# Where the search for the next part to begin ahead starts: at the part just split, or one past it

## The chip, the cores and the metric

One core of a Trainium2 chip runs the kernel. The metric is the device time of one execution in microseconds (us), and each row below is from one profiled execution. The engines are TensorE (PE: matmuls; PEld: its weight loads), VectorE (DVE), ScalarE (ACT), GpSimd (POOL) and SyncE (SP), which issues most of the DMAs.

## The reference

A decoder layer in float32 on 256 tokens of width 2048, with the rows of the two outer lines twice the size of the rest:

```python
x = x + 0.5 * swiglu(rms_norm(x, g_ffn1), w_gu1, w_down1)   # w_gu: 2048 x 2*5632, w_down: 5632 x 2048
x = x + hybrid_mixer(rms_norm(x, g_mix), ...)               # gated conv, windowed attention, w_o
x = x + 0.5 * swiglu(rms_norm(x, g_ffn2), w_gu2, w_down2)

def swiglu(h, w_gu, w_down):
    g, u = jnp.split(h @ w_gu, 2, axis=-1)
    return (jax.nn.silu(g) * u) @ w_down
```

## The kernel before

Each weight is read once, by SP, in **groups** of 128 x 2048 float32 (1 MB) into the tile `raw`, of which there are three. A group is cut into **parts** of at most 1024 columns. Each part is split into two tiles of the rounded type fp32r, `hi` (ACT copies it, L102) and `lo` = source minus `hi` (DVE subtracts, L103), and PE makes each product of three matmuls of 512 columns: x_hi*hi (L486), x_hi*lo (L487), x_lo*hi (L488).

The two SwiGLU half-steps run over 11 units of 512 columns of gate and up, in blocks of 4, 4 and 3; after each block come two down products. A unit has 8 pairs of 128-row blocks of the contraction. A pair is plain (`p`: two parts, eight products) or is made with seven products (`s`: sums of blocks first, four parts). `PLAN = "sppspspp"` sets this for units 2 to 10 (unit 2 in the order `FIRST`), `DOWN` for the down products; unit 0 is plain, and unit 1 has groups marked `q`. The four parts of an `s` group are taken in this order: `u` and `d`, 1024 columns each of sums that DVE makes from `raw` (L174 to L176); `a`, 1024 columns straight from `raw`; and `r`, 512 columns from `raw`. PE takes three products' worth of 512 columns less for them than for a plain pair, and DVE has the three sums more to do.

`Feed.take` hands PE its next part. Before that it goes on splitting parts as long as there are buffers: three `hi`/`lo` pairs in the pool `wsplit` (`BUFS`), one more in a late pool (`MORE`). So instructions of parts three or four ahead stand on ACT and DVE between those of the part at hand and the rest of the work. Other work is put in between from a list (`posts`, `pending`): the transposed activations (`act`, with the sums `rf` and `aforms`, for the down products), and at the end of a unit the **folds**: L544 to L548 gather what the seven products left, L552 to L555 add it to the four halves of the two PSUM tiles `mm`, L556 is silu, L558 the product. The next unit's third product writes into `mm` and so waits for L552 and L553.

There is a second way to split a part, meant for form `a` and for the second parts of `q` groups, with two buffers of its own (`ADDED`), which `take` does not count among the four:

```python
nc.scalar.copy(hi, src)                               # L185, tile ahi
nc.scalar.activation(lo, src, AF.Copy, scale=-1.0)    # L186, tile alo
nc.gpsimd.dma_start(lo, src, accum_op=ALU.add)        # L187, alo += src in the DMA
self.ready[i] = hi, lo, w, self.parts[i][3]
self.added += 1
```

`ahead(i)`, called right after part `i` was split in the ordinary way, looks from `begun` on for such a part in this group, or also in the next one when `i` isn't the first of its own. `added` goes down only when a part that `take` found ready is done with; where the part begun is `i` itself, its buffers are counted as ordinary ones and `added` stays up. With `added` at two, nothing is begun any more.

Of the kernel before, what the change touches and what calls it, by code (L numbers as in the profile page):

```python
# [56 lines left out]
def hybrid_layer(ctx: ExitStack, tc: tile.TileContext, a: dict, out: bass.AP):  # L57
# [67 lines left out]
    class Feed:  # L125
# [64 lines left out]

        def ahead(self, i):

            self.begun = max(self.begun, i)
            g = self.parts[i][0]
            first = i == 0 or self.parts[i - 1][0] != g
            for j in range(self.begun, min(i + 9, len(self.parts))):
                if self.parts[j][0] > g + (not first) or self.added == ADDED or not self.pool:
                    break
                self.begun = j + 1
                if self.parts[j][5] == "a":  # L200
                    self.begin(j)
# [840 lines left out]
```

## Time and profile before

| | |
|---|---|
| median of 3 runs (lowest to highest) | 2178.42 us (2176.48 to 2183.15) |
| profiled execution: time; span of its instructions | 2180.23 us; 2178.4 us |
| mean granted clock of PE | 0.977 |
| busy share: PE, DVE, ACT, POOL | 95%, 78%, 51%, 3% |
| parts begun ahead (L187 instructions) | 6 |

The rows take 0 to 800 us for the first half-step, 800 to 1440 for the mixer and its borders, and 1440 to the end for the second, less what little of it lies before. PE's busy time counts pipelined matmuls, so its idle time is a lower bound of what it loses, and a matmul at a lower granted clock counts as busy.

### The profile page before, as it was taken

How to read it: one execution, taken by the hardware profiler on the slowest of the kernel's cores; microseconds unless marked ns; L12 is line 12 of the kernel's file. 1: busy time of each engine (PE TensorE's matmuls, PEld its weight loads, DVE VectorE, ACT ScalarE, POOL GpSimd, SP SyncE). 2: the span in 40 equal slices, each digit the busy share in tenths (PEclk: the TensorE clock that was granted, in tenths of full speed). 3: DMA queues.
4: the chain of work that ended last, by engine and by line, in shares of the span. 5: the costliest groups of instructions: out<-in, count | busy, mean ns of one | idle time of the engine just before them, and what ended most of it. 6: DMA issues, size and time to landing. Idle time of an engine off the chain costs nothing. (4 is left out here: it accounts for less than half of the span.)

```text
span 2178.4 us, 24482 instructions
## 1 busy us (share of the span) xinstructions
PE 2067.9 (95%) x9482; PEld 1689.7 (78%) x9482; DVE 1689.0 (78%) x1912; ACT 1101.1 (51%) x1338; POOL 69.6 (3%) x61
## 2 busy tenths in 40 slices
PE   8889999999999999999999999998999999999998
PEld 7667787777877778887888888886778777787777
DVE  5678888888988874568766665658888888988887
ACT  5545555554555454455545444544544545545553
POOL 1000000000000000621000000000000000000000
PEclk9999999999999999999999999999999999999999
DMA  6655455444554445443555555554454545454444
GB/s 235 208 182 187 174 199 195 177 184 155 213 184 164 174 174 193 168 142 116 193 183 187 192 193 183 185 186 152 173 185 174 213 154 186 178 197 181 185 156 154
DMA packets 58230, 392.84 MB, mean 180 GB/s; under 512 B 6913, under 2 KB 8065, under 8 KB 12033
## 3 DMA queue, kind: packets, MB, share of 16 engines
q1 hardware_dynamic: 57104, 388.10, 49.3%
q0 software_dynamic: 864, 3.15, 0.8%
q8 instruction: 74, 1.21, 0.2%
q14 instruction: 44, 0.35, 0.1%
q10 hardware_dynamic: 144, 0.02, 0.0%
HBM read 386.00 MB, written 2.10 MB: 178 GB/s over the span
## 5 line engine op out<-in xcount | busy, mean ns | idle before, releaser
L103 DVE TENSOR_TENSOR lo<-raw,hi 128x1024 fp32r<-128x1024 f32 (+1 forms) x725 | 848.4, 1183 | 388.7 <-ACT hi L102 376.3
L102 ACT CAST hi<-raw 128x1024 fp32r<-128x1024 f32 (+1 forms) x725 | 718.5, 1000 | 498.4 <-PE mm L488 217.4
L486 PE MATMUL mm<-hi,h 128*128 128x512 f32 x955 | 380.5, 398 | 36.1 <-DVE v L553 31.3
L487 PE MATMUL mm<-lo,h 128*128 128x512 f32 x955 | 377.5, 395 | 8.0 <-DVE lo L103 7.9
L488 PE MATMUL mm<-hi,h 128*128 128x512 f32 x955 | 376.7, 394 | 0.0
L102 ACT CAST hi<-u 128x1024 fp32r<-128x1024 f32 x172 | 181.5, 1055 | 313.4 <-DVE u L174 275.9
L486 PEld LDWEIGHTS mm<-hi,h 128*128 128x128 f32 x955 | 181.9, 191 | 83.4 <-DVE v L553 36.6
L103 DVE TENSOR_TENSOR lo<-u,hi 128x1024 fp32r<-128x1024 f32 x172 | 210.1, 1222 | 13.8 <-ACT hi L102 10.0
L487 PEld LDWEIGHTS mm<-lo,h 128*128 128x128 f32 x955 | 181.9, 191 | 48.9 <-DVE lo L103 13.3
L488 PEld LDWEIGHTS mm<-hi,h 128*128 128x128 f32 x955 | 181.7, 190 | 38.7 <-DVE h L325 0.6
L486 PE MATMUL mm<-hi,act 128*128 128x512 f32 x512 | 202.8, 396 | 3.2 <-DVE v L555 1.9
L487 PE MATMUL mm<-lo,act 128*128 128x512 f32 x512 | 200.7, 392 | 0.0
L488 PE MATMUL mm<-hi,act 128*128 128x512 f32 x512 | 200.3, 391 | 0.0
L283 PE MATMUL gate<-h,hi 128*128 128x512 f32 x512 | 181.0, 396 | 0.0
L285 PE MATMUL gate<-h,lo 128*128 128x256 f32 x480 | 134.6, 280 | 0.0
L486 PEld LDWEIGHTS mm<-hi,act 128*128 128x128 f32 x512 | 97.2, 190 | 28.0 <-issue 4.4
L283 PEld LDWEIGHTS gate<-h,hi 128*128 128x128 f32 x512 | 96.0, 188 | 22.0 <-issue 0.8
L488 PEld LDWEIGHTS mm<-hi,act 128*128 128x128 f32 x512 | 96.9, 189 | 20.5
L487 PEld LDWEIGHTS mm<-lo,act 128*128 128x128 f32 x512 | 97.0, 189 | 19.7
L174 DVE TENSOR_TENSOR u<-raw 128x1024 f32<-128x1024 f32 x86 | 104.9, 1219 | 0.0
L283 PE MATMUL xc<-h,hi 128*128 128x512 f32 x256 | 93.1, 406 | 0.0
L285 PEld LDWEIGHTS gate<-h,lo 128*128 128x128 f32 x480 | 90.7, 189 | 0.7
(258 smaller groups left out, 3013.2 us busy)
## 6 DMA issues: line engine op xcount, KB each, us to landing
raw<-in_w_gu SPq DMA_DIRECT2D x172, 1024.0 KB, 4.6
raw<-in_w_down SPq DMA_DIRECT2D x88, 1024.0 KB, 4.7
raw<-in_w_mix SPq DMA_DIRECT2D x56, 1024.0 KB, 5.1
raw<-in_w_o SPq DMA_DIRECT2D x16, 1024.0 KB, 4.8
raw<-in_w_qkv SPq DMA_DIRECT2D x12, 1024.0 KB, 4.8
raw<-in_w_oc SPq DMA_DIRECT2D x8, 1024.0 KB, 4.8
raw<-in_w_oa SPq DMA_DIRECT2D x8, 1024.0 KB, 4.8
raw<-in_w_gu SPq DMA_DIRECT2D x7, 512.0 KB, 6.7
```

What stands on the lines that cost most here:

```text
L102: nc.scalar.copy(dst[0], src)
L103: nc.vector.tensor_tensor(dst[1], src, dst[0].bitcast(F32), op=ALU.subtract)
L174: nc.vector.tensor_tensor(u[:, :2], b[:, 0:4:3], b[:, 1:2].broadcast_to([P, 2, NCH]), op=ALU.add)
L283: nc.tensor.matmul(ps[:, b], whi, both, start=k == 0, stop=last)
L285: nc.tensor.matmul(ps[:, b, :S], wlo, x[:, k, 0], start=False, stop=False)
L486: nc.tensor.matmul(ps, x[0], hi, start=name not in self.begun, stop=False)
L487: nc.tensor.matmul(ps, x[0], lo, start=False, stop=False)
L488: nc.tensor.matmul(ps, x[1], hi, start=False, stop=last)
```

## The change

`ahead` begins its search one part later, so that it never begins the part that has just been split:

```diff
         def ahead(self, i):
 
-            self.begun = max(self.begun, i)
+            self.begun = max(self.begun, i + 1)
             g = self.parts[i][0]
             first = i == 0 or self.parts[i - 1][0] != g
             for j in range(self.begun, min(i + 9, len(self.parts))):
```

Two of the six parts begun before were the part at hand (in units 1 and 2 of the first half-step), and after them `added` stood at two for good. Now none is, and 94 parts are begun, 47 in each half-step, nearly all of the 102 of that kind. Past unit 1 each stands 6 to 8 parts ahead of the one that PE takes then.

ACT, where unit 7 of the second half-step goes over into the first down product (`g<-p` is the gather, `act` the turned activations, `hi<-u` the parts `u` and `d`, 1024 columns of `raw` the parts `p` and `a`, 512 columns `r`). Before:

```order
L544 COPY g<-p_13719 128x512
L102 CAST hi<-raw 128x1024
L102 CAST hi<-u 128x1024
L102 CAST act<-at 128x2x256
L102 CAST hi<-u 128x1024
L102 CAST act<-at 128x2x256
L102 CAST hi<-raw 128x1024
L556 ACTIVATE g<-g 128x1024
L102 CAST hi<-raw 128x512
```

And of the change:

```order
L544 COPY g<-p_13778 128x512
L102 CAST hi<-raw 128x1024
L185 CAST ahi<-raw 128x1024
L186 ACTIVATE alo<-raw 128x1024
L102 CAST hi<-u 128x1024
L102 CAST act<-at 128x2x256
L102 CAST hi<-u 128x1024
L185 CAST ahi<-raw 128x1024
L186 ACTIVATE alo<-raw 128x1024
L102 CAST act<-at 128x2x256
L102 CAST hi<-raw 128x512
L556 ACTIVATE g<-g 128x1024
```

Ahead of `hi<-u` stand two more instructions, for the `a` of this group, and behind the second `hi<-u` two for the `a` of the next; the copy of `a` in front of silu (L556) is gone, and that of `r` has moved ahead of silu.

DVE at the same place. Before:

```order
L103 TENSOR_TENSOR lo<-u,hi 128x1024
L103 TENSOR_TENSOR act<-at,act 128x2x256
L103 TENSOR_TENSOR lo<-u,hi 128x1024
L103 TENSOR_TENSOR act<-at,act 128x2x256
L103 TENSOR_TENSOR lo<-raw,hi 128x1024
L552 TENSOR_TENSOR g<-g,mm 128x512
L553 TENSOR_TENSOR v<-mm,v 128x512
L554 TENSOR_TENSOR g<-g,mm 128x512
L555 TENSOR_TENSOR v<-mm,v 128x512
L103 TENSOR_TENSOR lo<-raw,hi 128x512
L558 SCALAR_TENSOR_TENSOR g<-g,v 128x1024
L174 TENSOR_TENSOR u<-raw 128x1024
```

And of the change:

```order
L103 TENSOR_TENSOR lo<-u,hi 128x1024
L103 TENSOR_TENSOR act<-at,act 128x2x256
L103 TENSOR_TENSOR lo<-u,hi 128x1024
L103 TENSOR_TENSOR act<-at,act 128x2x256
L103 TENSOR_TENSOR lo<-raw,hi 128x512
L552 TENSOR_TENSOR g<-g,mm 128x512
L553 TENSOR_TENSOR v<-mm,v 128x512
L554 TENSOR_TENSOR g<-g,mm 128x512
L555 TENSOR_TENSOR v<-mm,v 128x512
L174 TENSOR_TENSOR u<-raw 128x1024
L175 TENSOR_TENSOR u<-u,raw 128x512
L176 TENSOR_TENSOR u<-u,raw 128x512
```

The subtraction for `a` in front of the folds (L552 to L555) is replaced with the shorter one for `r`, and the sums for the next group (L174) follow at once on the folds; L558 comes later.

DVE, where unit 4 of the second half-step goes over into unit 5. Before:

```order
L103 TENSOR_TENSOR lo<-u,hi 128x1024 x2
L103 TENSOR_TENSOR lo<-raw,hi 128x1024
L552 TENSOR_TENSOR g<-g,mm 128x512
L553 TENSOR_TENSOR v<-mm,v 128x512
L554 TENSOR_TENSOR g<-g,mm 128x512
L555 TENSOR_TENSOR v<-mm,v 128x512
L103 TENSOR_TENSOR lo<-raw,hi 128x512
L558 SCALAR_TENSOR_TENSOR g<-g,v 128x1024
L103 TENSOR_TENSOR lo<-raw,hi 128x1024 x4
```

And of the change:

```order
L103 TENSOR_TENSOR lo<-u,hi 128x1024 x2
L103 TENSOR_TENSOR lo<-raw,hi 128x512
L552 TENSOR_TENSOR g<-g,mm 128x512
L553 TENSOR_TENSOR v<-mm,v 128x512
L554 TENSOR_TENSOR g<-g,mm 128x512
L555 TENSOR_TENSOR v<-mm,v 128x512
L103 TENSOR_TENSOR lo<-raw,hi 128x1024
L558 SCALAR_TENSOR_TENSOR g<-g,v 128x1024
L103 TENSOR_TENSOR lo<-raw,hi 128x1024 x3
```

Again `r` stands ahead of the folds in the place of `a`, and the first plain part of the next group comes ahead of L558.

## Rows read from the trace of the kernel before

**Rows 1.** The page: the chain that ended last, by engine.
```profile
PE 22%; DVE 7%; ACT 1%; issue 1%; ACTq 0%
```

**Rows 2.** Stretches: us, busy us by engine (x instructions), granted clock, DMA share, GB/s.
```profile
140.00:800.00 660.00, 623.51 (x2695) 503.98 (x2694) 571.14 (x621) 338.42 (x382) 0.00 (x0) 0.97 0.50 183
800.00:1440.00 640.00, 636.86 (x3355) 535.36 (x3354) 397.44 (x469) 319.17 (x447) 55.45 (x42) 1.00 0.51 177
1440.00:1510.00 70.00, 61.34 (x258) 49.52 (x257) 55.51 (x80) 33.19 (x44) 0.00 (x0) 0.93 0.37 136
1510.00:2178.00 668.00, 627.21 (x2698) 506.74 (x2696) 572.36 (x617) 333.64 (x367) 0.00 (x0) 0.97 0.49 180
```

**Rows 3.** PE waiting for whom: us in total, times, longest us.
```profile
PE mm L486 <- DVE v L553: 32.5, 14, 4.9
PE p L486 <- ACT hi L102: 16.2, 6, 2.7
PE p L487 <- DVE lo L103: 13.1, 17, 0.9
PE mm L487 <- DVE lo L103: 7.9, 8, 1.7
...
PE gu L487 <- DMA alo<-raw: 5.6, 4, 2.7
```

**Rows 4.** DVE in order of time: start us, us, operation; [idle before <- releaser].
```profile
1761.55 0.68 DVE L545 TENSOR_TENSOR g<-g,p 128x512 f32<-128x512 f32 x1
...
1776.95 1.22 DVE L103 TENSOR_TENSOR lo<-raw,hi 128x1024 fp32r<-128x1024 f32 x1 [0.26 <-ACT hi L102]
1778.10 0.68 DVE L552 TENSOR_TENSOR g<-g,mm 128x512 f32<-128x512 f32 x1
```

**Rows 5.** ACT in order of time around the same place.
```profile
1747.76 1.06 ACT L102 CAST hi<-raw 128x1024 fp32r<-128x1024 f32 x1 [0.30 <-PE mm L488]
...
1760.28 0.58 ACT L544 COPY g<-p 128x512 f32<-128x512 f32 x1
...
1766.78 1.06 ACT L102 CAST hi<-u 128x1024 fp32r<-128x1024 f32 x1 [4.97 <-DVE u L174]
...
1775.88 1.04 ACT L102 CAST hi<-raw 128x1024 fp32r<-128x1024 f32 x1
```

**Rows 6.** PE in order of time, two matmuls that waited.
```profile
1879.05 0.50 PE L486 MATMUL p<-hi,aforms 128*128 128x512 f32 x1 [2.69 <-ACT hi L102]
1880.48 0.80 PE L487 MATMUL p<-lo,aforms 128*128 128x512 f32 x1 [0.93 <-DVE lo L103]
```

**Rows 7.** DVE in order of time at that place.
```profile
1874.88 0.69 DVE L103 TENSOR_TENSOR lo<-raw,hi 128x512 fp32r<-128x512 f32 x1 [1.04 <-ACT hi L102]
...
1876.62 1.22 DVE L174 TENSOR_TENSOR u<-raw 128x1024 f32<-128x1024 f32 x1
```

**Rows 8.** Short stretches, columns as in Rows 2.
```profile
1778.00:1785.00 7.00, 5.57 (x13) 4.25 (x14) 5.97 (x9) 4.55 (x6) 0.00 (x0) 0.51 0.24 84
1829.20:1832.60 3.40, 3.40 (x10) 2.60 (x8) 2.83 (x3) 3.40 (x5) 0.00 (x0) 0.50 0.32 87
1872.00:1880.50 8.50, 4.35 (x17) 2.30 (x15) 7.34 (x11) 3.71 (x5) 0.00 (x0) 1.00 0.35 123
2008.00:2016.00 8.00, 6.68 (x29) 5.05 (x28) 7.38 (x7) 4.39 (x6) 0.00 (x0) 1.00 0.64 229
```

**Rows 9.** Tile alo: xcount, duration ns min/median/max, first and last start us; landing.
```profile
L186 ACT ACTIVATE alo<-raw x6: 1048/1059/1069, 55.8 to 124.3; 128x1024 fp32r<-128x1024 f32 x6
...
DMA to landing us min/median/max: 4.5/4.6/7.7
```

**Rows 10.** POOL in order of time, one of the six issues.
```profile
77.10 0.85 POOL L187 DMA_DIRECT2D alo<-raw  x1 [16.23 <-ACT alo L186]
```

**Rows 11.** DVE in order of time beside it.
```profile
77.04 0.69 DVE L357 TENSOR_TENSOR rn<-h 128x512 f32<-128x512 f32 x1
```

**Rows 12.** PE in order of time, a matmul on the `lo` of `a`.
```profile
1757.98 0.39 PE L487 MATMUL mm<-lo,h 128*128 128x512 f32 x1
```


## The prediction

> **What bounds the kernel now.** I read the page first, then the stretches, then the waits of PE, then single places. PE is busy 95% of the span, yet 7% of the span lies on DVE in the chain that ended last, and 1% each on ACT and on issue [rows 1]. By stretches PE loses almost nothing in the mixer (636.86 of 640.00 us busy at clock 1.00), and much in the half-steps: 660.00 - 623.51 = 36.5 us idle from 140 to 800, 668.00 - 627.21 = 40.8 from 1510 on, at a mean clock of 0.97 in both [rows 2]. The clock has two levels, 2.4 and 1.2 GHz; a mean of 0.97 is worth 0.03 x 660 = 20 us in the one and as much in the other. So some 77 us of idleness and 40 us of slow clock are there to be had, besides the first units of each half-step (0 to 140 and 1440 to 1510).
>
> The waits say who ends this idleness. The four rows with DVE and ACT sum to 32.5 + 16.2 + 13.1 + 7.9 = 69.7 us [rows 3], nine tenths of the 77. They fall on the same twelve places in each half-step: where one unit follows another, where the down products follow a unit, and where the second down product follows the first. The reason is to be seen at one of them: DVE goes from the gather at 1761.55 through sums, subtractions and activations, and comes to the subtraction for `a` at 1776.95 and to the folds only at 1778.10 [rows 4]; the longest wait for L553, 4.9 us, ends there. ACT meanwhile stands idle 4.97 us ahead of 1766.78 for DVE's sums [rows 5].
>
> **What the change removes and adds.** 94 parts less 6 are begun ahead. Each takes a subtraction of 1.22 us from DVE [rows 4] and gives ACT 1.06 us more (L186; L185 stands for the L102 that goes), 0.85 us to POOL [rows 10], and a DMA of 512 KB that lands 4.5 to 7.7 us after its issue [rows 9]. Summed, DVE loses 88 x 1.22 = 107 us and ACT gains 93, but only what stands ahead of a PE wait counts, since elsewhere DVE and ACT wait for buffers anyway. ACT's extra two instructions mostly stand right ahead of `hi<-u`, where it idles for DVE's sums (4.97 us against 2.1), so there I cost them at nothing; without that cover each would delay `hi<-u` by 2.1 us.
>
> *Unit to unit with activations turned, eight places* (of the 32.5 us 4.9 at four places and about 2.9 at four; the other six waits are of 0.2). The copy and subtraction for `r` (0.69 us for the subtraction, at 1874.88 [rows 7]; the copy of 512 columns I set at 0.6, a little over half of 1.04) stand in the place of 1.04 and 1.22 for `a`. `hi` of `r` can start when ACT is done with `act`, 1775.88 + 0.1, DVE is free about 1776.7, so the folds start near 1777.25 and not at 1778.10: 0.85 us. Besides, `a` no longer holds one of four buffers, so the plain parts behind it are split one small part (1.36 us of PE) earlier, and the gather L545 follows not on three subtractions (1761.55) but on ACT's copy, which ends at 1760.86 [rows 4, 5]: 0.7 us more. That gives 1.55 each, 12.4 us; 0.85 each (6.8) if the second does not pass through.
>
> *Into the down products, six places.* From 1872 to 1880.5 PE is idle 8.50 - 4.35 = 4.15 us [rows 8], 2.69 and 0.93 of it in two waits [rows 6]. The long one is for `u` of the next `s` group, whose sums start at 1876.62, behind `r` (itself behind silu, at 1874.88) and L558 [rows 7]. Now the sums follow on the folds at once: 1876.62 - 3.3, and ACT's `hi` of it comes after silu at about 1875.7, when PE arrives. Against this, here alone two extra ACT instructions stand ahead of `act`, and with it of the folds: 2.1 us of ACT, all but 0.25 of it beside DVE's own work ahead of the folds; the earlier gather takes 0.7 off. What I then count at this place is about 0.3 for L555, 1.1 for `lo` of `u` and 1.0 for `lo` of `d`, which now stands behind L558: 2.4 us. Gain 1.75 each, 10.5 us; 1.05 each (6.3) without the earlier gather.
>
> *Second down product, six places* (0.9 us each, within the 13.1) and *unit to unit with nothing turned, four places* (from 2008 on 8.00 - 6.68 = 1.3 us idle [rows 8], most of the 7.9 [rows 3]). In the first 1.22 us leaves the chain ahead of the late `lo`; in the second `r` and L558 (0.69 + 1.22) no longer stand between the folds and the late `lo`. Both waits are shorter than what leaves (L558 runs 1.22 us, as the subtraction does), so they go: 5.4 + 5.2 = 10.6 us.
>
> *First units.* In the first half-step PE waited 5.6 us for `alo` in unit 1 [rows 3], on parts begun at hand or four parts ahead; now the nearest are five ahead. But two that had left DVE come back to it. I take 4. In the second half-step 8.7 us are idle from 1440 to 1510 [rows 2], and four subtractions (4.9 us) leave DVE there, against four more ACT instructions in a chain that goes to and fro between the two: I take 3. Sum 7, bounds 0 and 5.6 + 4.9 = 10.5.
>
> *Clock.* After the wait of 4.9 us PE ran 7 us at clock 0.51, after one of 2.9 us 3.4 us at 0.50; across the 1.3 us it stayed at 1.00 [rows 8]. So the 2.9 us places, at about 1.4 us, should stay at full clock, the 4.9 us ones at 3.4 should do as the 2.9 ones did, and the down places, in pieces of about 1 us, may go either way. I take half of the 40 us back, 20; bounds 0 and 30.
>
> *Late landings.* The tightest place in the steady part is the third `s` group of a unit. PE wants `lo` of `a` at 1757.98 [rows 12]. `ahi` would follow on the copy that starts at 1747.76 [rows 5], or 1.36 us earlier with the buffer freed one part earlier: 1.06 + 2.1 us later POOL issues, at 1750.9 or 1749.6, and a landing after 7.7 us is at 1758.6 or 1757.3: 0.6 us late, or in time. After 4.5 us it is in time either way. DMA is at a share of 0.50 [rows 2], so many landings will share the engines with a load of `raw`; I expect 5 to 8 us, and set 3 us for late ones at these 18 places; bounds 0 and 18 x 0.6 = 11. The loads of `raw` themselves are slowed too, but they go out two groups ahead.
>
> **Sum.** 12.4 + 10.5 + 10.6 + 7 + 20 - 3 = 57.5 us off 2180.2, the profiled execution's own time (0.08% over the median of the runs): 2123. Of the bounds, 6.8 + 6.3 + 10.6 + 0 + 0 - 11 = 13 give 2167, and 12.4 + 10.5 + 10.6 + 10.5 + 30 - 0 = 74 give 2106.
>
> **Rivals.** *The waits shorten but the clock does not come along, or landings eat part of it:* 13 to 30 us, 2150 to 2167. For it: the pieces that stay at the down places add up, and the 4.9 us places remain over 3. Chance 0.20.
>
> *Nothing moves:* the folds are late for ACT's activations and not for `a`, and PE waits as before; 2178. Against it: at 1776.95 the subtraction for `a` is the last thing ahead of the folds, and it is gone. Chance 0.06.
>
> *Slower: `alo` lands after PE wants it.* The four waits on it in unit 1 took 5.6 us, 1.4 each [rows 3]. If the accumulating DMAs and the loads hold each other up so that half of the 94 parts wait 1.4 us, that is 66 us against the gain of 57 (and the slow clock comes with such waits): 2190 to 2210. It decides from about 0.6 us a part, which at the tightest place means landings of 9 us, 1.3 over the longest seen. Chance 0.09.
>
> A rule speaks for this one: the Trainium skill, "SBUF — State Buffer", section "SBUF: two separate sides", says that GpSimd writes the descriptors of a DMA issued from its queue through ports that it shares with VectorE, and is locked out while certain VectorE instructions run, so that such a DMA waits for descriptors. By it, with DVE busy 86% of the half-steps, each landing would be put off by an instruction or two of DVE, 1.2 to 2.4 us: at the 18 tight places up to 1.7 us late, 31 us, so 2154. By this trace it doesn't hold for the instructions that DVE runs here: the issue at 77.10 fell 0.06 us into a DVE instruction with two SBUF inputs and another followed [rows 10, 11], and it took the usual 0.85 us. I leave it 0.03.
>
> **Chances and range.** The forecast (2106 to 2150) gets 0.62, the partial gain 0.20, the lock 0.03, no move 0.06, slower 0.09. Range 2100 to 2168, which leaves out no change and slower, and a little at the bottom. About 0.3%, 6.5 us, is what a measurement here can tell from nothing: faster 0.85, same 0.06, slower 0.09.
>
> **What would show it.** The subtraction L103 from `raw` is run 88 times less and L187 94 times. Each landing of `alo` within 8 us and PE's waits on it under 5 us in all. The waits on L553 fall from 32.5 to about 19 us, those on `hi` (16.2) to near nothing, those on `lo` in plain matmuls (7.9) too. The mean clock rises from 0.977 to about 0.985. I am wrong if PE's waits on `alo` go into tens of us, if ACT's extra copies appear ahead of `hi<-u` in PE's waits, or if PE's idle time falls and the clock doesn't rise.

## The result, and the profile after

The changed kernel takes 2112.29 us (median of 3 runs, 2107.99 to 2114.93) against 2178.42: a ratio of 0.969, interval 0.9654 to 0.9725, 66 us faster. Timed again (x_after, on a chip numbered 10; the chip of the first timing isn't on record) it took 2124.07 us (4 runs, 2119.46 to 2128.66; ratio 0.9747, 0.973 to 0.9764), where the kernel before took 2179.23. The forecast of 2123 and its range hold for both. The profiled execution of the first took 2114.93 us, with a span of 2113.1 us at a mean granted clock of 0.990 (0.977 before).

The page of the changed kernel: busy time by engine, the two large DMA queues (packets, MB, share of 16 engines), and the chain that ended last, which answers to [rows 1]:

```profile
PE 2044.4 (97%) x9482; PEld 1675.5 (79%) x9482; DVE 1586.0 (75%) x1822; ACT 1178.5 (56%) x1424; POOL 145.4 (7%) x149
...
q1 hardware_dynamic: 57104, 388.10, 51.3%
q0 software_dynamic: 13536, 49.29, 12.7%
...
PE 66%; DVE 15%; DMA 8%; ACT 5%; issue 5%; POOL 1%; SPq 0%; ACTq 0%; POOLq 0%; DVEq 0%
```

DVE is 103 us less busy than before (1689.0), ACT 77 us more (1101.1). PE's idle time (span less busy time) fell from 2178.4 - 2067.9 = 110.5 to 68.7 us, and its busy time by 23.5. The share of DVE and DMA in the chain has grown all the same: the chain goes back through whatever released each step, at no matter how small a wait, and so its shares are no measure of loss.

Stretches of the changed kernel, columns as in [rows 2, 8]; the last two lie behind the fold's wait at a change of unit with activations turned, and at a change to the down products:

```profile
140.00:800.00 660.00, 641.33 (x2825) 522.21 (x2825) 537.96 (x603) 391.11 (x450) 34.40 (x40) 0.99 0.71 223
800.00:1400.00 600.00, 596.86 (x3175) 502.19 (x3174) 376.98 (x437) 296.20 (x415) 55.50 (x42) 1.00 0.51 177
1400.00:1480.00 80.00, 72.42 (x303) 57.54 (x303) 58.61 (x84) 44.15 (x55) 5.16 (x6) 0.96 0.62 191
1480.00:2113.00 633.00, 608.48 (x2673) 494.50 (x2671) 516.99 (x568) 366.72 (x403) 35.25 (x41) 0.99 0.70 221
1732.60:1736.00 3.40, 3.18 (x8) 2.44 (x8) 1.94 (x3) 3.40 (x4) 0.00 (x0) 0.51 0.53 222
1823.00:1831.00 8.00, 6.43 (x25) 4.17 (x24) 7.93 (x10) 6.64 (x8) 0.00 (x0) 1.00 0.48 160
```

From 140 to 800 PE is idle 18.7 us where it was 36.5, and 24.5 us in the second half-step behind its first units where it was 40.8; the mixer's 3.1 us are as before. The DMA engines' share has risen from 0.50 to 0.71.

Who PE waits for in the changed kernel (us, times, longest), to be set against [rows 3]:

```profile
PE mm L486 <- DVE v L553: 19.1, 8, 3.8
PE p L487 <- DVE lo L103: 9.5, 13, 0.9
PE p L486 <- ACT g L566: 7.0, 2, 3.6
PE mm L487 <- DMA alo<-raw: 6.9, 8, 1.8
PE mm L487 <- DVE lo L103: 4.4, 5, 1.8
...
PE gu L487 <- DMA alo<-raw: 0.6, 2, 0.4
```

The 16.2 us on `hi` in the down products are gone. DVE in order of time at one change of unit, and then at one change to the down products, which answer to [rows 4, 7]:

```profile
1729.24 0.69 DVE L103 TENSOR_TENSOR act<-rn,act 128x512 fp32r<-128x512 f32 x1
1729.85 0.68 DVE L103 TENSOR_TENSOR lo<-raw,hi 128x512 fp32r<-128x512 f32 x1
1730.45 0.68 DVE L552 TENSOR_TENSOR g<-g,mm 128x512 f32<-128x512 f32 x1
...
1823.05 0.68 DVE L555 TENSOR_TENSOR v<-mm,v 128x512 f32<-128x512 f32 x1
1823.65 1.21 DVE L174 TENSOR_TENSOR u<-raw 128x1024 f32<-128x1024 f32 x1
...
1826.24 1.22 DVE L103 TENSOR_TENSOR lo<-u,hi 128x1024 fp32r<-128x1024 f32 x1
1827.37 1.22 DVE L558 SCALAR_TENSOR_TENSOR g<-g,v 128x1024 f32<-128x1024 f32 x1
```

And PE there, with one of the new waits on a landing:

```profile
414.29 0.50 PE L487 MATMUL mm<-alo,h 128*128 128x512 f32 x1 [1.83 <-DMA alo<-raw]
...
1731.78 0.50 PE L486 MATMUL mm<-hi,h 128*128 128x512 f32 x1 [3.84 <-DVE v L553]
...
1827.51 0.50 PE L487 MATMUL p<-lo,aforms 128*128 128x512 f32 x1 [0.92 <-DVE lo L103]
...
1829.78 0.50 PE L487 MATMUL p<-lo,aforms 128*128 128x512 f32 x1 [0.60 <-DVE lo L103]
```

The short subtraction for `r` stands ahead of the folds now, the sums for the next group begin 0.6 us after L555 does, and what is left at the down place is 1.57 us where it was 4.15. Tile `alo` of the changed kernel, as in [rows 9]:

```profile
L187 POOL DMA_DIRECT2D alo<-raw x94: 850/859/1018, 57.3 to 2074.2; - x94
...
DMA to landing us min/median/max: 4.5/6.7/10.3
```

### The profile page after: what moved, and what is told of

Same layout as the page of the kernel before. It is cut to its first block, busy times and chain, and to the rows that moved or that the text cites. A ratio compares the mean times of both kernels' runs of the same rounds, so it can differ in the third digit from the quotient of the medians.

```text
span 2113.1 us, 24661 instructions
## 1 busy us (share of the span) xinstructions
PE 2044.4 (97%) x9482; PEld 1675.5 (79%) x9482; DVE 1586.0 (75%) x1822; ACT 1178.5 (56%) x1424; POOL 145.4 (7%) x149
## 3 DMA queue, kind: packets, MB, share of 16 engines
q0 software_dynamic: 13536, 49.29, 12.7%
## 4 chain that ended last, share of the span: by engine, by line
PE 66%; DVE 15%; DMA 8%; ACT 5%; issue 5%; POOL 1%; SPq 0%; ACTq 0%; POOLq 0%; DVEq 0%
PE mm L487 11%; PE mm L488 11%; PE mm L486 11%; PE gate L283 6%; DVE lo L103 5%; DMA alo<-raw 5%; PE yo L283 3%; PE gate L285 3%; ACT hi L102 2%; DMA raw<-in_w_gu 2%; PE p L487 2%; PE xc L283 2%; PE p L488 2%; PE p L486 2%; PE bg L283 2%
## 5 line engine op out<-in xcount | busy, mean ns | idle before, releaser
L103 DVE TENSOR_TENSOR lo<-raw,hi 128x1024 fp32r<-128x1024 f32 (+1 forms) x635 | 742.1, 1177 | 397.8 <-ACT hi L102 387.4
L102 ACT CAST hi<-raw 128x1024 fp32r<-128x1024 f32 (+1 forms) x635 | 623.6, 990 | 484.3 <-PE mm L488 192.3
L486 PE MATMUL mm<-hi,h 128*128 128x512 f32 x902 | 358.0, 397 | 23.1 <-DVE v L553 19.1
L487 PE MATMUL mm<-lo,h 128*128 128x512 f32 x902 | 354.5, 393 | 4.9 <-DVE lo L103 4.4
L488 PE MATMUL mm<-hi,h 128*128 128x512 f32 x902 | 354.3, 393 | 0.0
L102 ACT CAST hi<-u 128x1024 fp32r<-128x1024 f32 x172 | 181.2, 1054 | 161.8 <-DVE u L174 117.1
L486 PEld LDWEIGHTS mm<-hi,h 128*128 128x128 f32 x902 | 171.4, 190 | 63.3 <-DVE v L553 22.5
L103 DVE TENSOR_TENSOR lo<-u,hi 128x1024 fp32r<-128x1024 f32 x172 | 209.9, 1220 | 13.4 <-ACT hi L102 10.3
L488 PEld LDWEIGHTS mm<-hi,h 128*128 128x128 f32 x902 | 170.8, 189 | 36.2 <-DVE h L325 0.4
L187 POOL DMA_DIRECT2D alo<-raw x94 | 81.0, 862 | 1686.7 <-ACT alo L186 1611.6
L486 PE MATMUL mm<-hi,act 128*128 128x512 f32 x480 | 187.8, 391 | 0.0
L488 PE MATMUL mm<-hi,act 128*128 128x512 f32 x480 | 186.9, 389 | 0.0
L487 PE MATMUL mm<-lo,act 128*128 128x512 f32 x480 | 186.8, 389 | 0.0
L488 PEld LDWEIGHTS mm<-hi,act 128*128 128x128 f32 x480 | 90.1, 188 | 18.8
L486 PEld LDWEIGHTS mm<-hi,act 128*128 128x128 f32 x480 | 90.1, 188 | 18.6 <-DVE v L553 0.2
L174 DVE TENSOR_TENSOR u<-raw 128x1024 f32<-128x1024 f32 x86 | 104.7, 1217 | 0.0
L185 ACT CAST ahi<-raw 128x1024 fp32r<-128x1024 f32 x94 | 98.5, 1048 | 5.1 <-DMA raw<-in_w_gu 3.7
```

Source lines behind the costliest of these rows:

```text
L102: nc.scalar.copy(dst[0], src)
L103: nc.vector.tensor_tensor(dst[1], src, dst[0].bitcast(F32), op=ALU.subtract)
L174: nc.vector.tensor_tensor(u[:, :2], b[:, 0:4:3], b[:, 1:2].broadcast_to([P, 2, NCH]), op=ALU.add)
L486: nc.tensor.matmul(ps, x[0], hi, start=name not in self.begun, stop=False)
L487: nc.tensor.matmul(ps, x[0], lo, start=False, stop=False)
L488: nc.tensor.matmul(ps, x[1], hi, start=False, stop=last)
```

## The experiments

The question is what made the time: the subtractions that DVE is rid of (relief), or the two buffers that `take` doesn't count, by which six parts and not four can be in hand (depth). Every edit is to the changed kernel. Four kernels ran on each of three chips; the kernel before took 2178.42, 2178.71 and 2179.23 us there. Times are medians of at least four runs (of three in the first two rows); idle is PE's span less its busy time in the profiled run.

| label | what is different | us | ratio to before, interval | clock | idle us | PE's waits on alo, us |
|---|---|---|---|---|---|---|
| (before) | | 2178.42 | | 0.977 | 110.5 | 8.9 |
| (after) | the change, first timing | 2112.29 | 0.9654 to 0.9725 | 0.990 | 68.7 | 7.5 |
| x_none | nothing begun ahead | 2173.53 | 0.9968 to 0.9986 | 0.977 | 104.2 | 0 |
| x_depth | begun ahead, DVE subtracts | 2127.78 | 0.9753 to 0.9782 | 0.989 | 80.9 | 0 |
| x_counted | begun parts count among the four (98 begun) | 2143.02 | 0.9824 to 0.9857 | 0.985 | 86.2 | 12.8 |
| x_act2 | L186 twice | 2141.20 | 0.9818 to 0.9847 | 0.989 | 86.9 | 12.2 |
| x_first | first groups alone | 2119.86 | 0.9712 to 0.9741 | 0.988 | 70.6 | 0.9 |
| x_rest | all but the first groups | 2174.40 | 0.9971 to 0.9992 | 0.978 | 109.4 | 8.5 |
| x_near | search 3 parts ahead, not 9 | 2157.83 | 0.9889 to 0.9919 | 0.989 | 95.6 | 14.2 |
| x_keep | some products made twice | 2118.63 | 0.9706 to 0.9751 | 0.994 | 65.7 | 10.7 |
| x_after | the changed kernel again | 2124.07 | 0.9730 to 0.9764 | 0.991 | 76.1 | 13.8 |
| x_more | three ordinary late pairs, none begun | 2127.69 | 0.9753 to 0.9782 | 0.989 | 84.6 | 0 |
| x_mix | DMA in first groups, DVE elsewhere | 2105.33 | 0.9648 to 0.9676 | 0.990 | 62.2 | 1.9 |
| x_planq | 112 parts begun | 2186.00 | 1.0023 to 1.0046 | 0.975 | 118.0 | 15.6 |

### x_none

```diff
-ADDED = 2
+ADDED = 0
```

(`ahi` and `alo` get the number 2 for their buffers, which are never made.)

> The changed kernel with no part begun ahead at all (ADDED = 0), so that all subtractions are on VectorE and nothing goes wrong in unit 1. Relief theory (the gain is VectorE's subtractions that left the chain ahead of the folds): about the time of before, 2165 to 2185 us, VectorE busy near 1690 us. Fault theory (the six parts begun before did the harm, by the waits on alo and two buffers held for good): near the changed kernel, 2105 to 2130. Depth theory (the two buffers that take does not count let the split run further ahead): 2165 to 2185, as relief.

2173.53 us, with the waits of the kernel before:

```profile
PE mm L486 <- DVE v L553: 32.4, 14, 4.9
PE p L486 <- ACT hi L102: 16.2, 6, 2.7
```

The six parts that the kernel before began cost it 5 us, all of it in the first units; the rest of the gain is something that the change brings. Two of those six were begun after they had been split, so they were split twice: L103 from `raw` runs 725 times before and 635 after, 90 fewer and not 88.

### x_depth

```diff
-            nc.scalar.activation(lo, src, AF.Copy, scale=-1.0)
-            nc.gpsimd.dma_start(lo, src, accum_op=ALU.add)
+            nc.vector.tensor_tensor(lo, src, hi.bitcast(F32), op=ALU.subtract)
```

> As the changed kernel, with the same 94 parts begun ahead in the same buffers, but alo is made by VectorE's subtraction and not by the second ScalarE instruction and the accumulating DMA. Relief theory: the gain is gone, 2160 to 2190 us, since each subtraction only stands earlier in the same chain; the waits on L553 stay above 28 us in all. Depth theory: most of the gain stays, 2110 to 2135.

2127.78 us: 46 of the 61 us between x_none and the first timing of the changed kernel come without one subtraction leaving DVE (1691.3 us busy, x_none 1693.2). Against x_none PE's idle time falls by 23.3 us and its busy time by 21.7. Two rows of its waits:

```profile
PE mm L485 <- DVE v L552: 31.1, 14, 4.0
PE p L486 <- DVE lo L103: 14.7, 23, 0.9
```

And PE at one change to the down products:

```profile
1831.86 0.50 PE L485 MATMUL mm<-hi,act 128*128 128x512 f32 x1 [1.02 <-DVE v L552]
```

The waits at the change of unit stay (L552 is here what L553 is elsewhere), but none of them is 4.9 long, and the 2.7 us waits on `hi` at the down products are gone, and with them the stretches of low clock behind them. So the depth theory holds, and the relief theory fails on the time, though the waits on the fold stay above 28 us as it said. One part of the gain is missing here: at the changes to the down products PE waits 1.0 us for the fold, where it waited 0.2 us in the kernel before and has no wait on L553 in the changed one.

### x_counted

```diff
             while self.split < len(self.parts):
+                if len(self.homes) >= BUFS + MORE:
+                    break
```

(It stands behind the branch for parts that are ready.)

> As the changed kernel, but the parts begun ahead count among the four that may be split ahead, so that the depth is that of before and VectorE is relieved all the same. Relief theory: most of the gain stays, and what goes is the earlier gather, 0.7 us at 14 places, and a little clock: 2118 to 2140 us; the wait ahead of the folds at the four long places is near 4.5 us and not 3.8. Depth theory: 2160 to 2180.

2143.02 us, between what the two theories gave and 30 us better than x_none: relief with little depth (a part that is begun and not yet reached by `split` is still not counted). The 16.0 us on `hi` at the down products stay in this one:

```profile
PE mm L488 <- DVE v L555: 17.1, 8, 3.4
PE p L488 <- ACT hi L102: 16.0, 6, 2.7
```

So relief shortens the change of unit, and depth removes the wait on `hi` ahead of the down products. Alone they give 30 and 46 us, together 49 to 61: they overlap, and what is put down to each depends on which is taken first. Relief adds 4 to 15 us where depth is there already, and depth 19 to 31 where relief is.

### x_act2

```diff
             nc.scalar.activation(lo, src, AF.Copy, scale=-1.0)
+            nc.scalar.activation(lo, src, AF.Copy, scale=-1.0)
```

> As the changed kernel, but the second ScalarE instruction of each part begun ahead is issued twice (the second writes the same): 94 x 1.06 = 100 us more on ScalarE. If ScalarE's extra work is hidden in its wait for VectorE's sums (about 5 us at the unit ends, 2.5 within a unit), the time rises by at most 15 us, to 2113 to 2128, mostly at the down products, where two of them stand ahead of the activations. If ScalarE is close to being the bound, most of the 100 us shows: 2160 to 2215.

2141.2 us. 94 more instructions of 1.05 us, 99 us of ACT in all, cost 17 us against x_after and 29 against the first timing, more than the 15 expected of a hidden instruction. PE's waits show where: 23.8 us on the fold, 15.3 on `lo` in the down products and 12.2 on landings, against 19.1, 9.5 and 7.5 in the first timing. "Costed at nothing" was too little for one more; what the present two cost is bounded by this and was not measured by itself.

### x_first and x_rest

```diff
-                if self.parts[j][5] == "a":
+                if self.parts[j][5] == "a" and self.parts[j][3] == 0:
```

(x_first, 34 parts: the first group of each unit and down product. x_rest has `!= 0`: the other 60.)

> As the changed kernel, but of the parts only those are begun ahead whose group is the first of a unit or of a down product (34 parts, all three of unit 2 among them); the others go the ordinary way. Relief theory in the form that only what stands ahead of a PE wait counts: most of the gain from a third of the parts, 2120 to 2145 us. If every subtraction taken off VectorE counts alike, 34/94 of the 66 us: about 2155.

> The complement: the parts of all other groups are begun ahead (60), those of the first group of a unit or down product go the ordinary way. Relief theory in the form that only what stands ahead of a PE wait counts: little of the gain, 2145 to 2172 us, with the waits on L553 at 25 us or more. If every subtraction counts alike, 60/94 of 66 us: about 2136.

2119.86 and 2174.40 us. A third of the parts gives nearly the whole gain, and two thirds of them give what x_none gives. x_rest lies 2 us above the range expected, with 31.0 us of waits on the fold. Buffers and subtractions go together in these two runs, so they show where the change counts, around the places where PE waits, and not which of the two counts there; x_mix below takes them apart.

### x_near

```diff
-            for j in range(self.begun, min(i + 9, len(self.parts))):
+            for j in range(self.begun, min(i + 3, len(self.parts))):
```

> As the changed kernel, but a part is begun only when it is at most two parts beyond the one at hand (i + 3 for i + 9): the two ScalarE instructions then stand behind the copy of u, and not ahead of it where ScalarE waits for the sums, and the DMA has some 3 us less. If lead and cover are what make the DMA way free: PE's waits on alo rise from 7.5 us to 40 or more, the time to 2150 to 2200 us. If they don't matter: 2108 to 2120.

2157.83 us. PE's waits on `alo` come to 14.2 us and not to the 40 and more that I had expected, yet idle time is 95.6 us:

```profile
PE mm L486 <- DVE v L553: 26.7, 11, 4.0
PE p L487 <- DVE lo L103: 17.2, 23, 0.9
...
L103 DVE TENSOR_TENSOR lo<-u,hi 128x1024 fp32r<-128x1024 f32 x172 | 210.1, 1221 | 100.1 <-ACT hi L102 99.9
```

Beginning the parts early is worth 34 to 46 us, and PE's waits on landings explain 0 to 7 of it; much of the rest lies at the folds and at `lo`. All 94 parts are begun here too (L187 runs 94 times). What differs is ACT's order: at the places read, the two extra instructions stand between the copies of `u` and `d`, and the last row shows DVE idle 99.9 us for these copies, where it is 10.3 in the changed kernel. That this is what costs the time was not tried by itself.

### x_keep

```diff
+                    if self.again and p == self.order[0] and name in ("p5", "p6", "p7"):
+                        self.product(name, x[name], hi[:, js], lo[:, js], True)
+                        self.begun.discard(name)
                     self.product(name, x[name], hi[:, js], lo[:, js], last and name[0] == "p")
```

(`again` is set in units 6 and 10: three products that need no fold are made twice there, the first time to no use, so that PE has work in the place of the wait.)

> As the changed kernel, but in units 6 and 10 of each half-step, whose first folded product waits 3.8 us for VectorE, the three products ahead of that wait (p5, p7, p6 of the first group, nine matmuls, 2 us at full clock) are made twice, the first time for nothing. If the slow clock after these four waits comes from the waiting, it stays at full there, and 5 to 8.5 us are gained (17 us at half clock in all): 2104 to 2108 us; if the clock has nothing to do with it, the time is that of the changed kernel within 3 us, the extra matmuls being hidden in the wait.

2118.63 us: between the two timings of the changed kernel, so no gain where 2104 to 2108 were expected. The waits on the fold are 11.5 us with a longest of 1.8, and the mean clock is 0.994, the highest of all runs:

```profile
PE mm L486 <- DVE v L556: 11.5, 8, 1.8
```

The clock rises where the waits are filled. That the 36 added matmuls and the waits on `alo` took what it gave back is argued from these rows and not shown.

### x_after, x_more, x_mix, x_planq

These four ran on one chip.

x_after is the changed kernel.

> The changed kernel itself once more, so that the next three can be set against it on one chip. Every theory expects 2107 to 2116 us.

It missed: 2124.07 us, 12 over the first timing, with the kernel before within 1 us in both. The waits on `alo` are 13.8 us where they were 7.5:

```profile
PE mm L487 <- DMA alo<-raw: 12.6, 13, 2.6
...
DMA to landing us min/median/max: 4.5/7.8/11.1
```

x_more:

```diff
-MORE = 1
-ADDED = 2
+MORE = 3
+ADDED = 0
```

> Nothing is begun ahead, and the late pool has three ordinary pairs of hi and lo in the place of one (no ahi and alo): as many parts in hand as in the changed kernel, but split in the order in which PE takes them. If two more buffers are what counts, this comes to the time of the kernel that begins the parts and subtracts on DVE, 2120 to 2140 us. If it is that a is split early and out of turn, so that less stands ahead of the folds on DVE, this gains nothing, since six parts and not four then stand ahead of the folds: 2170 to 2200 us, with waits for L553 of 30 us or more.

2127.69 us, x_depth's time to 0.1 us, with no part begun out of turn. So two more buffers of any kind do it, and the order in which `a` comes is not needed. The waits are others, though:

```profile
PE p L486 <- ACT g L566: 17.9, 2, 8.9
PE mm L486 <- DVE v L553: 15.0, 14, 2.9
PE at L114 <- DVE g L545: 12.4, 14, 0.9
PE at L114 <- ACT g L679: 8.3, 6, 2.2
PE at L114 <- ACT g L544: 5.9, 14, 0.4
PE at L114 <- DVE g L680: 4.3, 6, 0.7
```

With six parts in turn more splits stand ahead of the gather (L544, L545), and the transposes wait for it, 30.9 us in the four rows; the folds come earlier against what PE does (2.9 us at the longest), and the waits on `hi` and `lo` in the down products are gone. The first row lies at two places in the first units and was 7.0 us in the changed kernel, so the units behind them gain more than the whole time shows.

x_mix:

```diff
+            if self.parts[i][3] == 0:
                 nc.scalar.activation(lo, src, AF.Copy, scale=-1.0)
                 nc.gpsimd.dma_start(lo, src, accum_op=ALU.add)
+            else:
+                nc.vector.tensor_tensor(lo, src, hi.bitcast(F32), op=ALU.subtract)
```

> All 94 parts are begun ahead; in the first group of a unit or down product alo is made by ACT and the accumulating DMA, in the other groups DVE subtracts it (no DMA). If DVE's relief counts only around the changes of unit, and the late landings of the rest cost something, 2106 to 2114 us, with PE's waits on alo under 2 us. If the relief counts in the other groups too, 2116 to 2126 us.

2105.33 us, 18.7 under the changed kernel on the same chip (the intervals are far apart) and the fastest of all. It has the depth of x_depth and relief in the first groups alone:

```profile
PE mm L489 <- DVE v L556: 19.7, 8, 3.8
PE p L490 <- DVE lo L103: 10.2, 14, 0.9
```

The 34 accumulating DMAs where PE waits are worth 22 us against x_depth and x_more; the 60 others, with their second instruction on ACT and less what they spare DVE, cost 19 on this chip, with 12 us more of waits on `alo` (13.8 against 1.9). Against x_first, which begins the same 34 and no others, the 60 begun for their buffers alone give another 15 us (on two chips).

x_planq:

```diff
-PLAN = "sppspspp"
+PLAN = "sppspspq"
```

> The changed kernel with the last pair of PLAN taken as q: the second plain part of each unit is begun ahead too, 112 parts in all and not 94. If relief of DVE ahead of the folds is still worth what it was, each unit change gains another subtraction of 1.2 us, some 10 to 15 us: 2098 to 2104 us. If the buffers and the landings bind by now, 2110 to 2125 us, with PE's waits on alo above 10 us.

2186.0 us, slower than the kernel before, and neither expectation holds: PE's waits on landings are only 15.6 us. Its waits on the fold, and DVE and then PE at one change of unit:

```profile
PE mm L486 <- DVE v L553: 67.1, 18, 6.6
...
1782.44 0.69 DVE L103 TENSOR_TENSOR act<-rn,act 128x512 fp32r<-128x512 f32 x1
1783.39 1.23 DVE L103 TENSOR_TENSOR lo<-raw,hi 128x1024 fp32r<-128x1024 f32 x1 [0.25 <-ACT hi L102]
1784.53 0.68 DVE L552 TENSOR_TENSOR g<-g,mm 128x512 f32<-128x512 f32 x1
...
1785.86 0.80 PE L486 MATMUL mm<-hi,h 128*128 128x512 f32 x1 [6.55 <-DVE v L553]
```

DVE has less to do than in any other run (1570.2 us), and the waits are the longest. One part begun more lets the four ordinary buffers reach one part further: the small subtraction for `r` comes before the last activations, and a whole 1024-column subtraction of a plain part stands directly ahead of the folds, as it did in the kernel before. The rows show what stands there; that the further reach of the buffers put it there follows from the order of the program and was not tried by itself.

## Why the prediction was right

**The sum.** Forecast were 57.5 us, 37.5 of waits and 20 of clock. The profiled executions differ by 65.3 us of span: 41.8 of idle time and 23.5 of busy time. By the mean clock the loss to the low level was 0.023 x 2178 = 50 us and is 0.010 x 2113 = 21, so 29 less; part of a slow stretch lies within a wait, though, and costs nothing there, so the 23.5 of busy time is the fairer measure of the 20. Where it came from was in part missed: [rows 8] end at 1880.5, and the slow stretch behind the wait into the down products begins there.

```profile
1880.40:1883.80 3.40, 3.32 (x8) 2.64 (x9) 2.99 (x4) 2.29 (x4) 0.00 (x0) 0.50 0.00 0
```

Such a stretch of 3.4 or 6.8 us followed at all six of these places (30.7 us together, some 15 lost), and none does in the changed kernel. The forecast had left these places open. That the second timing, 2124.07, meets the 2123 is chance: the waits gave more than forecast, and the landings took more.

**Unit to unit, activations turned.** 1.55 us each, 12.4 in all, were forecast; the eight waits on L553 fell from 31.3 to 19.1, by 12.2. The folds come directly after the subtraction for `r`, as worked out. That the sum fits so closely is luck: the four long waits fell by 1.1 us each (4.92 to 3.8, where 3.4 was given), the four short ones by 1.8 to 2.4 (2.9 to between 0.5 and 1.1, where 1.4 was given). Behind three of the long ones 3.4 us at the low clock are left and not 7; behind the one that ends at 651.64 it is near 6 still. Behind the short ones there is none.

**Into the down products.** 2.4 us were to be left of 4.15; left are 1.57 (0.92 and 0.60), so 15.5 us in all and not 10.5. The wait that I priced for L555 isn't in PE's rows at this place, and the one on the second `lo` is 0.60, not 1.0. x_counted and x_depth show what carried it. With relief alone the waits on `hi` stay at 16.0 us, so the further reach of the splits removed these and not DVE's time. With depth alone 2.8 us are left at such a place, 1.0 of it on the fold, so some 1.4 us of the gain are depth's and 1.2 relief's.

**Second down product, and unit to unit with nothing turned.** 10.6 us were forecast. At the second down products the waits of 0.9 us on `lo` are gone from all six (5.5 us); PE waits for `alo` at three of them instead (0.4 to 0.8 us, counted with the landings). Of the second kind this is one wait of four in the kernel before:

```profile
2011.64 0.51 PE L487 MATMUL mm<-lo,h 128*128 128x512 f32 x1 [1.32 <-DVE lo L103]
```

All four are gone (5.3 us); the 4.4 us left on `lo` in plain matmuls lie in the first units, where 2.5 were before. So 10.8 us, as forecast. In x_depth these four are gone too, so here DVE's relief wasn't needed.

**First units.** In the first half-step PE is idle 14.7 us from 0 to 140 where it was 21.0, 6.3 less against 4 (the kernel before also waited 3.3 us for `alo` in unit 2, which [rows 3] do not show); in the second 7.6 us are idle from 1400 to 1480 where 8.7 were from 1440 to 1510, so 1.1 and not 3. The stretches are not quite the same, so this is rough; 7.4 in all against 7.

**Late landings.** Named as at most 8 us each and under 5 us of waiting; they took up to 10.3 and made PE wait 7.5 us, and 13.8 in the second timing, which comes near the forecast's own sign of being wrong (tens of us). This step was mis-sized, and most of what separates the two timings lies here: of the 8.8 us between the two spans 6.3 are in these waits. For the steady part 3 us were priced, with a bound of 11; 6.9 and 12.6 were measured. One of these waits cost clock as well (1.83 us at 414.29, and 0.50 from 415.2 to 418.5). x_mix shows a net cost of 19 us for the parts begun by DMA where PE doesn't wait. The rival on this side (half of the parts 1.4 us late) wanted 47 waits; 10 and 15 came, of 0.8 and 0.9 us in the mean.

**The waits together.** 12.2 + 15.5 + 10.8 + 7.4 - 6.9 = 39.0 of the 41.8 us of idle time; the rest lies in waits of under half a microsecond that the forecast did not price. (The 69.7 us of [rows 3] are of the whole span, and some lie in the first units; the 77 leave these out.) 37.5 were forecast, so a gain too small at the down products and a price too small for the landings cancel in part.

**ACT at nothing.** One more instruction on ACT costs 17 to 29 us (x_act2), so the cover is thinner than the 4.97 us of [rows 5], at one place, made it look. In all ACT's idle time ahead of `hi<-u` for DVE's sums was 275.9 us (85 waits, 3.2 in the mean), and is 117.1 in the changed kernel and 50.6 in x_act2. What the two instructions themselves cost was not measured.

**What the prediction said of the cause.** The steps at the places were those that the trace shows, but I took them to come from DVE's relief, except for 0.7 us at fourteen places that I gave to the buffer that `a` no longer holds. That fell: the time was right and the credit was not. Taken in this order, the runs give 5 us to the six parts begun before, 46 to two more buffers (x_none to x_depth or x_more, the same time by either), and 4 (on the chip of x_more) to 15 to relief after what the landings cost. Taken the other way, relief has 30 us (x_counted) and depth 19 to 31. Had the change merely given two more ordinary buffers, it would have been worth 51 us.

**The rule on the SBUF ports.** The section that the prediction names (the Trainium skill, "SBUF — State Buffer", "SBUF: two separate sides") puts this lockout down to VectorE instructions in a two-port mode; the prediction let it hold for all that DVE runs, which gave 2154. The 94 issues took 0.85 to 1.02 us with DVE 75% busy, the same as the one in [rows 10]: for these instructions the trace does not show it. What lengthened the landings goes with the loads of `raw`. By the trace's times of issue and landing, the 14 accumulating DMAs that went out with no load under way landed in 4.5 to 6.2 us (median 5.4), the 30 that went out with two under way in 6.3 to 10.3 (7.7). In x_near, at as many bytes, a landing overlaps such loads by 0.4 us in the median, in the changed kernel by 5.0, and takes 4.5 us where it takes 6.7. No run moved the loads by themselves.

## What to carry to other kernels

Two kernels that differ in buffers and in work can't be told apart by the order of instructions alone: give the buffers without the work taken away before crediting the relief. Move work off an engine only at the places where the bound engine waits for it (34 parts of 94 here), and leave the rest where it is, since the other way costs too. After every change of depth, read again what stands directly ahead of the instruction that is waited for: with 18 more parts begun (x_planq) a 1.2 us subtraction stood in front of the folds again, and the kernel was 62 us slower than the changed one.

## What the runs showed of the hardware

The accumulating DMA of 512 KB from one tile into another lands after 4.5 us at best, 6.7 or 7.8 in the middle (4.5 in x_near) and 10 to 11 at worst, beside loads that take 51 to 53% of the engines' time; its 94 instances take 12.0 to 12.7% of that time for 49.29 MB. The same kernel differs by 12 us between two timings in which a kernel without many of them differs by 1; whether it is the chip was not tried, since the first one isn't on record.

The granted clock stayed at its upper level, 2.4 GHz, across 1.57 us of idling out of 8 (1823 to 1831, clock 1.00), and fell to 1.2 GHz after single waits of 3.84 us and after one of 1.83 us (at 414.29). In x_keep the same four waits are 1.8 us long. Its clock behind the one that ended at 1734.15, and behind the one that ended at 2001.11:

```profile
1734.00:1741.00 7.00, 6.49 (x26) 4.76 (x27) 5.54 (x7) 6.27 (x7) 0.00 (x0) 1.00 0.39 140
2003.00:2006.50 3.50, 3.50 (x11) 2.68 (x10) 2.79 (x3) 3.15 (x4) 0.00 (x0) 0.52 0.25 103
```

It stays up behind three of the four and falls behind the last.
